# A two-layer encoder trunk on one core: the MLP's first tile pairs, its spills and its block order

## The chip, the cores and the metric

One Trainium2 chip, one of its cores. The metric is the device time of one launch in microseconds (us). The five engines are TensorE (PE, with its weight loads as PEld), VectorE (DVE), ScalarE (ACT), GpSimd (POOL) and SyncE (SP, which here issues every DMA).

## The reference, cut to what matters

```python
D_MODEL, SEQ, DEPTH, D_FF = 1024, 1024, 2, 4096
for l in range(DEPTH):
    h = rms_norm(x, norm1_g[l])
    ...                                   # attention and recurrence heads -> mixed
    x = x + jnp.einsum('bsc,cd->bsd', mixed, w_out[l])
    h2 = rms_norm(x, norm2_g[l])
    u = jax.nn.relu(jnp.einsum('bsd,df->bsf', h2, w_up[l]))
    x = x + jnp.einsum('bsf,fd->bsd', u * u, w_down[l])
return rms_norm(x, final_g)
```

Everything is float32. The change lies in the second half of a layer: the output projection's norm, the up product with its squared ReLU, and the down product.

## The kernel before, in words

Activations lie transposed, with 128 features on the partitions and the sequence along the free axis in two halves of 512 (`hf` 0 and 1). A float32 product is made of three matmuls: each operand is split into a rounded high part (`hi`) and the rest (`lo`), and hi·hi, hi·lo and lo·hi are added in PSUM. A split is one ACT cast and one DVE subtraction (L543 and L544 for activations, L599 and L600 for weights).

Both MLP products use Strassen's scheme in Winograd's form: 7 block products in place of 8. A left block A11 to A22 is 128x128 of weights, a right block B11 to B22 is 128x512 of activations; the row index is the feature block, the column index the half of the sequence. The weight sums S1 to S4 are formed on POOL in `lhs_forms` (L591 and L610), the activation sums T1 to T4 in `strassen_rhs` for the up product. `up_pair` makes a *pair* q, two 128-wide tiles of the 4096 hidden features; 16 pairs make the hidden layer. Its 7 products have 4 blocks of depth and 3 matmuls each: 84 matmuls. They run in the order A11·B11, A12·B21, S2·T2, S1·T1, S3·T3, S4·B22, A22·T4, on three accumulators `a`, `b`, `c` (PSUM tags `pa`, `mm`, `pr`). Partial sums leave `a` and `c` by `copy_out` (ACT, L640); `fin` finishes three of the four outputs with two DVE instructions (L655 adds, L656 does ReLU and square in one) and the fourth with two ACT instructions (L652, L653).

`spill(q, ...)` forms the T sums of the pair's squared outputs on POOL (L679 to L687) and writes all seven forms to DRAM (`us`). When all 16 pairs are done, the 16 x tiles are read back (L885), and the down product reads the forms with `fetch_rhs` (L694), seven per q, and splits them. A *block* (t, q0, n) of the down product (`down_pair`) adds n of the 16 depth steps to two tiles of the output: 7 products of 3n matmuls, each followed by one DVE addition into x (L705). A product on the same accumulator as the one before it waits until that addition has read it. The order is three short blocks (n = 1, 2, 3), twelve of n = 4, and four that close a row of tiles each: (0,12,4), (1,13,3), (2,14,2), (3,15,1). These four defer their S1 and S4 products (`tail`), so that the first half of x is finished first; `leave` then norms that half while the tails run.

The order of the instructions on each engine is fixed when the program is built: the instructions are placed in the order of the text, with those in `tc.high_priority()` first, by a model of when each is ready. An engine, and SP's queue of DMAs, then takes them strictly in that order. Tiles with the same tag share `bufs` slots: the tag `us` has 6 slots of 128x512, for partial sums, spilled sums and fetched forms. The split tiles of the up product's right side (B11[k], T2[k], ... for k = 0 to 3) are the same memory as those of the down product (`form_tiles(f, q % 4)`), so a fetched form can be split only when the last pair has read that form.

Of the kernel before, what the change touches and what calls it, by code (L numbers as in the profile page):

```python
# [38 lines left out]
US = 6  # L39


@with_exitstack
def trunk(ctx, tc, x, norm1_g, w_in, lam_qk, attn_norm_g, lb_logits, hgrn_norm_g,
# [136 lines left out]
    def sum_squares(sqp, xt, hf):  # L180
        acc = half(sqp, "sqa", 1)
        A.activation(acc, xt[0][hf], AF.Square)
        for b in range(1, NB):
            sq = half(sqp, "sq", 2)
# [13 lines left out]
    def norm_rows(sqp, xt, hf):  # L198
# [6 lines left out]
        inv_sqrt(R, acc, half(sqp, "sq", 2))  # L205
# [352 lines left out]
    def strassen_rhs(hst, h, mp):  # L558

        B = [{"B11": hst[k], "B21": hst[k + 4]} for k in range(4)]  # L560
        t2 = []
        for k in range(4):
            b11, b12, b21, b22 = h[k]
            V.tensor_tensor(b11, b12, b11, op=ALU.subtract)
            t = half(mp, "us", US)
            V.tensor_tensor(t, b22, b11, op=ALU.subtract)
            t2.append(t)
            B[k]["T2"] = split_into(form_tiles("T2", k, mp), t)
        for k in range(4):
            b11, b12, b21, b22 = h[k]  # L570
            B[k]["T1"] = split_into(form_tiles("T1", k, mp), b11)
        for k in range(4):
            b11, b12, b21, b22 = h[k]
            G.tensor_tensor(b12, b22, b12, op=ALU.subtract)
            B[k]["T3"] = split_into(form_tiles("T3", k, mp), b12)
        for k in range(4):
            B[k]["B22"] = split_into(form_tiles("B22", k, mp), h[k][3])
        for k in range(4):
            b21 = h[k][2]
            G.tensor_tensor(b21, b21, t2[k], op=ALU.subtract)  # L580
            B[k]["T4"] = split_into(form_tiles("T4", k, mp), b21)
        return B

    def lhs_forms(src, mp, view, n, part=0):

        with tc.high_priority():
            wr = mp.tile([P, 8, 256], F32, tag="wr", name="wr", bufs=2)
            dma(wr[:, :2 * n], src)
            v = wr[:, :2 * n].rearrange(view, i=2)
            c0, c1 = slice(0, P), slice(P, 2 * P)  # L590
            sub = lambda o, a, b: G.tensor_tensor(o, a, b, op=ALU.subtract)  # L591
            out = {}

            def group(names, x):
                m = len(names)
                hi = wp.tile([P, 1024], F32R, tag="whi", name="whi")
# [10 lines left out]
            sa, sb = stile(), stile()  # L607
            if part != 2:
                group(("A11", "A12"), v[:, :, :, c0])
            G.tensor_tensor(sa[:, 0], v[:, 0, :, c1], v[:, 1, :, c1], op=ALU.add)  # L610
            if part == 0:
                sub(sa[:, 1], sa[:, 0], v[:, 0, :, c0])
                group(("S1", "S2"), sa)
                sub(sb[:, 0], v[:, 0, :, c0], v[:, 0, :, c1])
                sub(sb[:, 1], v[:, 1, :, c0], sa[:, 1])
                group(("S3", "S4"), sb)
            elif part == 1:
                sub(sb[:, 0], sa[:, 0], v[:, 0, :, c0])
                sub(sb[:, 1], v[:, 0, :, c0], v[:, 0, :, c1])
                group(("S2", "S3"), sb)  # L620
            else:
                sub(sb[:, 0], sa[:, 0], v[:, 0, :, c0])
                sub(sa[:, 1], v[:, 1, :, c0], sb[:, 0])
                group(("S1", "S4"), sa)
            if part != 2:
# [3 lines left out]
    def product(ps, w, B, f, ks, start):  # L629
        n = len(ks)  # L630
        for j, k in enumerate(ks):
            hi, lo = B[k][f]
            for i, (lt, rt) in enumerate(((w[0], hi), (w[0], lo), (w[1], hi))):
                T.matmul(ps, lt[:, j], rt, start=(start and j + i == 0), stop=(j == n - 1 and i == 2),  # L634
                         skip_group_check=True)

    def copy_out(mp, ps):
        t = half(mp, "us", US)
        with tc.high_priority():
            A.copy(t, ps)  # L640
        return t

    def up_pair(w, B, q, xtile, mp):

        ks = range(4)
        o = [xtile(4 * (q // 2 % 2) + i, q % 2) for i in range(4)]
        a, b, c = pst("pa"), mmp.tile([P, HALF], F32, tag="mm", name="mm"), pst("pr")

        def fin(i, ps, x):
            with tc.high_priority():  # L650
                if x is None:
                    A.activation(o[i], ps, AF.Relu)  # L652
                    A.activation(o[i], o[i], AF.Square)  # L653
                else:
# [4 lines left out]
        p1 = copy_out(mp, a)  # L659
        product(b, w["A12"], B, "B21", ks, True)  # L660
        fin(0, b, p1)
        product(a, w["S2"], B, "T2", ks, False)
        p6 = copy_out(mp, a)
        product(c, w["S1"], B, "T1", ks, True)
        p5 = copy_out(mp, c)
        product(a, w["S3"], B, "T3", ks, False)
        fin(3, a, p5)
        product(c, w["S4"], B, "B22", ks, False)
        fin(1, c, p6)
        product(a, w["A22"], B, "T4", ks, False)  # L670
        fin(2, a, None)
        return o

    def spill(q, u, mp):
# [4 lines left out]
        G.tensor_tensor(t1, u12, u11, op=ALU.subtract)  # L679
        put("T1", t1)  # L680
        put("B22", u22)
        G.tensor_tensor(t2, u22, t1, op=ALU.subtract)
        put("T2", t2)
        G.tensor_tensor(u12, u22, u12, op=ALU.subtract)
        put("T3", u12)
        put("B21", u21)
        G.tensor_tensor(t4, u21, t2, op=ALU.subtract)  # L687
        put("T4", t4)

    def fetch_rhs(q, mp):  # L690
        r = {}
        for i, f in enumerate(FORMS):
            t = half(mp, "us", US)
            dma(t, us[:, q, i])  # L694
            r[f] = split_into(form_tiles(f, q % 4, mp), t)
        return r

    def down_pair(w, B, q0, n, xt, t, defer=False):
        ks = range(q0, q0 + n)
        a, b, c = pst("pa"), mmp.tile([P, HALF], F32, tag="mm", name="mm"), pst("pr")  # L700

        def add(i, hf, ps):
            x = xt[2 * t + i][hf]
            with tc.high_priority():
# [253 lines left out]
```

## Time and profile before

| | us |
|---|---|
| median of 3 runs (lowest, highest) | 2696.88 (2689.63, 2703.72) |
| the profiled execution | 2696.91 |
| its span, first to last instruction | 2695.1 |
| busy: PE, PEld | 2501.1, 2060.9 |
| busy: DVE, ACT, POOL | 1830.3, 1161.5, 825.9 |

The mean granted TensorE clock is 0.964 of full speed. PE is busy for 93% of the span; the MLP of the first layer lies between about 645 and 1355 us, that of the second between about 1979 and 2690 us. Busy time counts pipelined matmuls by their modelled ends, so where matmuls stand back to back their distance (start to start), not their duration, is their price.

### The profile page before, as it was taken

The page shows a single profiled execution, that of the slowest core. Times are in us where ns is not written, and L with a number is a line of the kernel's source. Part 1 is how long each engine was busy: PE and PEld are TensorE (multiplying, and loading weights), DVE is VectorE, ACT ScalarE, POOL GpSimd, SP SyncE. Part 2 cuts the span into 40 slices and gives each one's busy share as a digit, 9 for nine tenths or more (in the row PEclk, how much of TensorE's full clock was granted, in tenths as well). Part 3 has the DMA queues.
Part 4 walks back from the last instruction along what each step waited for, and adds up shares of the span by engine and source line. Part 5 has one row for each costly group of instructions (what it writes and reads, how often), then busy time and mean ns, then how long its engine had stood idle before and what let it go on. Part 6 is the DMA issues. An engine that isn't in the chain of part 4 may idle for free. (4 is left out here: it accounts for less than half of the span.)

```text
span 2695.1 us, 34858 instructions
## 1 busy us (share of the span) xinstructions
PE 2501.1 (93%) x12640; PEld 2060.9 (76%) x12640; DVE 1830.3 (68%) x3177; ACT 1161.5 (43%) x2271; POOL 825.9 (31%) x508
## 2 busy tenths in 40 slices
PE   8999999986999979999899999998969999799996
PEld 6877887875788857788688778877758888578875
DVE  5567566867655559887745775588775555688875
ACT  5455445644333334433434554456433333344432
POOL 1111111003667553333311111110037666333322
PEclk9999999988999989999999999999989999899998
DMA  7111111152344556443421111112714445654433
GB/s 235 42 52 44 52 44 48 59 191 83 131 151 147 168 200 192 138 152 117 140 60 48 40 44 44 48 48 62 228 47 141 154 145 174 210 168 154 144 98 113
DMA packets 255884, 306.85 MB, mean 114 GB/s; under 512 B 13968, under 2 KB 166844, under 8 KB 255712
## 3 DMA queue, kind: packets, MB, share of 16 engines
q1 hardware_dynamic: 255712, 304.63, 34.8%
q8 instruction: 99, 1.62, 0.2%
q14 instruction: 73, 0.60, 0.1%
HBM read 213.33 MB, written 89.41 MB: 112 GB/s over the span
## 5 line engine op out<-in xcount | busy, mean ns | idle before, releaser
L634 PE MATMUL pa<-T,whi 128*128 128x512 f32 x1536 | 488.2, 399 | 20.7 <-DVE x L705 18.1
L610 POOL TENSOR_TENSOR wst<-wr 128x512 f32<-128x512 f32 (+3 forms) x78 | 113.9, 1461 | 917.0 <-DVE wlo L129 293.7
L129 POOL TENSOR_TENSOR wlo<-wst,whi 128x1024 fp32r<-128x1024 f32 x56 | 138.2, 2468 | 815.3 <-ACT whi L127 791.5
L143 PE MATMUL mm<-hh,whi 128*128 128x512 f32 x896 | 364.4, 407 | 1.2 <-DVE ta L747 0.9
L143 PE MATMUL mm<-hh,wlo 128*128 128x512 f32 x896 | 363.4, 406 | 1.7 <-POOL wlo L129 1.7
L634 PEld LDWEIGHTS pa<-T,whi 128*128 128x128 f32 x1536 | 289.8, 190 | 94.9 <-DVE x L705 12.5
L143 PE MATMUL mm<-hl,whi 128*128 128x512 f32 x896 | 361.3, 404 | 0.0
L634 PE MATMUL pa<-T,wlo 128*128 128x512 f32 x768 | 304.7, 397 | 0.0
L599 ACT CAST whi<-wr 128x1024 fp32r<-128x1024 f32 (+5 forms) x140 | 109.0, 779 | 314.7 <-PE pr L634 271.5
L599 ACT CAST whi<-wst 128x1024 fp32r<-128x1024 f32 (+3 forms) x140 | 137.0, 979 | 232.7 <-PE mm L634 89.6
L600 DVE TENSOR_TENSOR wlo<-wst,whi 128x1024 fp32r<-128x1024 f32 (+3 forms) x140 | 207.4, 1481 | 41.2 <-ACT whi L599 41.2
L634 PE MATMUL pr<-hh,whi 128*128 128x512 f32 x512 | 207.6, 406 | 25.9 <-ACT hh L543 19.4
L634 PE MATMUL pr<-hl,whi 128*128 128x512 f32 x512 | 203.5, 397 | 21.4 <-DVE hl L544 21.4
L634 PE MATMUL pr<-hh,wlo 128*128 128x512 f32 x512 | 203.4, 398 | 0.0
L600 DVE TENSOR_TENSOR wlo<-wr,whi 128x1024 fp32r<-128x1024 f32 (+5 forms) x140 | 163.0, 1164 | 54.2 <-ACT whi L599 53.9
L143 PEld LDWEIGHTS mm<-hh,wlo 128*128 128x128 f32 x896 | 172.2, 192 | 36.0 <-POOL wlo L129 4.0
L143 PEld LDWEIGHTS mm<-hl,whi 128*128 128x128 f32 x896 | 173.4, 193 | 33.8 <-issue 1.2
L143 PEld LDWEIGHTS mm<-hh,whi 128*128 128x128 f32 x896 | 172.9, 193 | 34.3 <-DVE ta L747 1.7
L634 PEld LDWEIGHTS pa<-T,wlo 128*128 128x128 f32 x768 | 146.0, 190 | 35.0
L543 ACT CAST hh<-us 128x512 fp32r<-128x512 f32 x128 | 79.2, 620 | 185.6 <-PE pr L634 100.9
L221 PE MATMUL mm<-wlo,hh 128*128 128x256 f32 x512 | 147.7, 288 | 0.3 <-POOL wlo L129 0.3
L221 PE MATMUL mm<-whi,hh 128*128 128x256 f32 x512 | 148.0, 289 | 0.0
(242 smaller groups left out, 5697.9 us busy)
## 6 DMA issues: line engine op xcount, KB each, us to landing
us<-us SPq DMA_DIRECT2D x320, 256.0 KB, 2.6
wr<-w_up SPq DMA_DIRECT2D x32, 1024.0 KB, 5.7
us<-x SPq DMA_DIRECT2D x128, 256.0 KB, 2.3
wst<-w_in SPq DMA_DIRECT2D x56, 512.0 KB, 3.7
wr<-w_down SPq DMA_DIRECT2D x28, 1024.0 KB, 4.8
wst<-w_out SPq DMA_DIRECT2D x32, 512.0 KB, 4.0
x<-xs SPq DMA_DIRECT2D x64, 256.0 KB, 4.0
xs<-x SPq DMA_DIRECT2D x48, 256.0 KB, 2.7
```

The source lines that it names most:

```text
L129: eng.tensor_tensor(lo, st, hi.bitcast(F32), op=ALU.subtract)
L143: T.matmul(ps, lt[:, b], rt, start=(i == 0), stop=(i == n - 1))
L221: T.matmul(ps[:, t * 256:t * 256 + 256], lt[:, tsl], rt[:, b], start=(i + t + b + k == 0), stop=(i == 1 and b == 3 and k == 2), skip_group ...
L543: A.copy(hl[0], src)
L599: A.copy(hv, x)
L600: V.tensor_tensor(lv, x, hv.bitcast(F32), op=ALU.subtract)
L610: G.tensor_tensor(sa[:, 0], v[:, 0, :, c1], v[:, 1, :, c1], op=ALU.add)
L634: T.matmul(ps, lt[:, j], rt, start=(start and j + i == 0), stop=(j == n - 1 and i == 2), skip_group_check=True)
```

## The change

- The pairs q = 0 and 1 of the up product are no longer made by Strassen's 7 products but by the plain 8 (`up_plain`), first for half 0 of the sequence (4 products for each pair), then for half 1. Their splits of half 1 lie in the tiles of B22 and T4, the weights of the second pair in the tiles of T3.
- `strassen_rhs` and `spill` form their sums with DVE instructions in place of POOL's, in place.
- Of each up pair, all four outputs take ReLU and square on ACT; DVE keeps the three additions (`squared`).
- Four x tiles and the first four forms of q = 0 are loaded ahead of the last pair, through a new tag `uf` with 4 slots; the splits and fetches of q = 0 and 1 stand in the text ahead of the last pair's spill. The other x tiles come after it.
- The down product starts with (0,0,2) and then runs (1,0,1) and (2,0,3) together, product by product (`down_pairs`); at the end (1,13,3) and (2,15,1) run together, between (3,12,4) and (0,14,2). The twelve blocks of n = 4 take the row of tiles t in the order 3, 1, 0, 2.
- All x tiles come from one pool; the squares of the norms use the tag `us` instead of tiles of their own.

The diff, cut to its core:

```diff
 def strassen_rhs(hst, h, mp):
+    B = [{"B11": hst[k, 0], "B21": hst[k + 4, 0], "B22": hst[k + 4, 1]} for k in range(4)]
+    sub = lambda o, x, y: V.tensor_tensor(o, x, y, op=ALU.subtract)
     for k in range(4):
         b11, b12, b21, b22 = h[k]
-        V.tensor_tensor(b11, b12, b11, op=ALU.subtract)
-        t = half(mp, "us", US)
-        V.tensor_tensor(t, b22, b11, op=ALU.subtract)
...
-        G.tensor_tensor(b12, b22, b12, op=ALU.subtract)
...
-        G.tensor_tensor(b21, b21, t2[k], op=ALU.subtract)
+        sub(b11, b12, b11)
+        sub(b12, b22, b12)
+        sub(b22, b22, b11)
+        B[k]["T2"] = split_into(form_tiles("T2", k, mp), b22)
     for k in range(4):
+        B[k]["T1"] = split_into(form_tiles("T1", k, mp), h[k][0])
+    for k in range(4):
+        sub(h[k][2], h[k][2], h[k][3])
+    for f, i in (("T3", 1), ("T4", 2)):
+        for k in range(4):
+            B[k][f] = split_into(form_tiles(f, k, mp), h[k][i])
...
+def up_plain(w, B, sfx, o):
+    for m in (1, 2):
+        ps = pst("pa") if m == 1 else mmp.tile([P, HALF], F32, tag="mm", name="mm")
+        product(ps, w[f"A{m}1"], B, "B1" + sfx, range(4), True)
+        product(ps, w[f"A{m}2"], B, "B2" + sfx, range(4), False)
+        squared(o[m - 1], ps, None)
+
+def squared(o, ps, x):
     with tc.high_priority():
-        A.copy(t, ps)
...
-                if x is None:
-                    A.activation(o[i], ps, AF.Relu)
-                    A.activation(o[i], o[i], AF.Square)
-                else:
-                    V.tensor_tensor(o[i], ps, x, op=ALU.add)
-                    V.scalar_tensor_tensor(o[i], o[i], 0.0, o[i], op0=ALU.max, op1=ALU.mult)
+        if x is None:
+            A.activation(o, ps, AF.Relu)
+        else:
+            V.tensor_tensor(o, ps, x, op=ALU.add)
+            A.activation(o, o, AF.Relu)
+        A.activation(o, o, AF.Square)
...
 def spill(q, u, mp):
...
-    G.tensor_tensor(t1, u12, u11, op=ALU.subtract)
+    V.tensor_tensor(t1, u12, u11, op=ALU.subtract)
...
+def down_pairs(w, B, windows, xt, defer=False):
...
+    def step(bk, wf, f, start, i, hf):
+        off = 0
+        for j, (t, q0, n) in enumerate(windows):
+            product(ps[j, bk], w[wf], B, f, range(q0, q0 + n), start, off)
+            off += n
+            x = xt[2 * t + i][hf]
+            with tc.high_priority():
+                V.tensor_tensor(x, ps[j, bk], x, op=ALU.add)
...
         for b in (0, 4, 1, 5, 2, 6, 3, 7):
...
-                if hf == 0:
-                    hst[b] = split_into(h_tiles(b, 0), xt[b][0])
+                hst[b, hf] = split_into(h_tiles(b, 0) if hf == 0 else form_tiles("B22", b - 4, mp)
+                                        if b >= 4 else form_tiles("T4", b, mp), xt[b][hf])
...
+        wP = [up_forms(0, "AB"), up_forms(1, "AB", [3, 2, 1, 0])]
+        oP = [[half(mp, "uf", UF) for _ in range(2)] for _ in range(2)]
+        for q in range(2):
+            up_plain(wP[q], hP, "1", oP[q])
+        for q in range(2):
+            o = [half(mp, "us", US) for _ in range(2)]
+            up_plain(wP[q], hP, "2", o)
+            oP[q] = [oP[q][0], o[0], oP[q][1], o[1]]
         hB = strassen_rhs(hst, ..., mp)
+        for q in range(2):
+            spill(q, oP[q], mp)
...
-        for q in range(NF // 2):
...
+        for q in range(2, NF // 2):
+            if q == NF // 2 - 1:
+                for b in range(4):
+                    load_x(b)
+                st = {}
+                fetch_rhs(0, mp, None, st, FORMS[:UF], "uf")
+            u2 = up_pair(up_forms(q, "AS2"), hB, q, xtile, mp)
+            if q == NF // 2 - 1:
+                for i in range(2):
+                    uB[i] = {}
+                    split_rhs(i, mp, uB[i], st)
+                    fetch_rhs(i, mp, None, st, [f for f in FORMS if f not in uB[i]][:UF], "uf")
+                    split_rhs(i, mp, uB[i], st)
+                    if i == 0:
+                        fetch_rhs(1, mp, None, st, FORMS[:UF], "uf")
             spill(q, u2, mp)
...
-        steps = [(1, 0, 1), (2, 0, 2), (3, 0, 3)]
-        steps += [(r % 4, r, 4) for r in range(13)]
-        final = [(0, 12, 4), (1, 13, 3), (2, 14, 2), (3, 15, 1)]
+        steps = [[(0, 0, 2)], [(1, 0, 1), (2, 0, 3)]] + [[((3, 1, 0, 2)[r % 4], r, 4)] for r in range(12)]
+        final = [[(3, 12, 4)], [(1, 13, 3), (2, 15, 1)], [(0, 14, 2)]]
```

## Rows read from the trace of the kernel before

**Rows 1.** Windows: width; busy (count) PE, PEld, DVE, ACT, POOL; PEclk, DMA, GB/s

```profile
645.00:713.80 68.80, 47.67 (x187) 36.93 (x186) 51.71 (x64) 27.14 (x42) 35.41 (x20) 0.80 0.21 69
713.80:981.30 267.50, 267.50 (x1165) 218.28 (x1163) 151.55 (x139) 89.05 (x123) 174.24 (x113) 1.00 0.46 159
981.30:1050.80 69.50, 47.28 (x176) 33.62 (x175) 54.39 (x71) 30.19 (x49) 25.08 (x18) 0.88 0.65 212
1050.80:1282.80 232.00, 231.58 (x995) 185.98 (x996) 189.12 (x213) 92.86 (x129) 78.02 (x46) 1.00 0.45 141
1282.80:1340.00 57.20, 47.49 (x182) 34.88 (x180) 38.23 (x60) 20.20 (x35) 15.91 (x18) 0.91 0.39 129
1979.00:2047.00 68.00, 46.86 (x188) 36.41 (x187) 51.92 (x64) 27.68 (x43) 36.38 (x21) 0.82 0.21 70
2313.80:2385.00 71.20, 48.41 (x177) 34.63 (x176) 54.40 (x71) 30.25 (x49) 25.86 (x18) 0.86 0.63 207
2615.00:2655.00 40.00, 32.46 (x136) 23.25 (x134) 23.83 (x35) 10.38 (x17) 8.69 (x11) 0.96 0.28 93
```

**Rows 2.** TensorE's waits, 570 to 1400 us: total, times, longest (us)

```profile
PE pa L634 <- ACT hh L543: 14.3, 1, 14.3
PE pr L634 <- DVE hl L544: 10.7, 1, 10.7
PE pr L634 <- ACT hh L543: 9.7, 1, 9.7
PE pa L634 <- DVE x L705: 8.5, 8, 1.7
```

**Rows 3.** Timeline of VectorE and GpSimd, first layer's second norm: start, duration (us)

```profile
649.74 0.69 DVE L203 TENSOR_SCALAR sqa<-pa 128x512 f32<-128x512 f32 x1 [1.22 <-PE pa L202]
655.45 5.39 DVE L830 SCALAR_TENSOR_TENSOR x<-x,cols,R 128x512 f32<-128x512 f32 x8
661.52 4.67 POOL L574 TENSOR_TENSOR x<-x,x 128x512 f32<-128x512 f32 x2 [10.60 <-DVE x L564]
675.78 0.68 DVE L544 TENSOR_TENSOR hl<-x,hh 128x512 fp32r<-128x512 f32 x1
```

**Rows 4.** Timeline of SP's DMAs and ScalarE, last pair's end to first fetches

```profile
982.73 1.72 SPq L677 DMA_DIRECT2D us<-us  x2
987.93 0.32 SPq L677 DMA_DIRECT2D us<-us  x1
988.30 1.87 SPq L885 DMA_DIRECT2D x<-xs  x4
990.22 9.37 SPq L694 DMA_DIRECT2D us<-us  x10
995.29 1.25 ACT L543 CAST hh<-us 128x512 fp32r<-128x512 f32 x2 [12.24 <-DMA us<-us]
```

**Rows 5.** Groups of VectorE, 995.9 to 1050.8 us: busy (us), mean (ns), idle before

```profile
L544 DVE TENSOR_TENSOR hl<-us,hh 128x512 fp32r<-128x512 f32 x19 | 19.6, 1043 | 13.0 <-ACT hh L543 13.0
L544 DVE TENSOR_TENSOR T<-us,T 128x512 fp32r<-128x512 f32 x13 | 11.3, 870 | 0.0
```

**Rows 6.** Groups of VectorE, up pairs of the first layer, 713.8 to 981.3 us

```profile
L600 DVE TENSOR_TENSOR wlo<-wst,whi 128x1024 fp32r<-128x1024 f32 x27 | 48.5, 1795 | 14.4 <-ACT whi L599 14.4
L656 DVE SCALAR_TENSOR_TENSOR x<-x 128x512 f32<-128x512 f32 x42 | 39.7, 946 | 1.4
L655 DVE TENSOR_TENSOR x<-pa,us 128x512 f32<-128x512 f32 x14 | 9.7, 692 | 13.4 <-PE pa L634 13.4
```

**Rows 7.** Groups of ScalarE, the same stretch

```profile
L653 ACT ACTIVATE x<-x 128x512 f32<-128x512 f32 x13 | 8.2, 634 | 0.4
L652 ACT ACTIVATE x<-pa 128x512 f32<-128x512 f32 x13 | 7.6, 588 | 0.0
```

**Rows 8.** Timeline of VectorE and ScalarE, a pair's end and the last sums

```profile
941.60 1.22 DVE L600 TENSOR_TENSOR wlo<-wr,whi 128x1024 fp32r<-128x1024 f32 x1
...
944.42 0.63 ACT L653 ACTIVATE x<-x 128x512 f32<-128x512 f32 x1
...
2680.38 0.68 DVE L705 TENSOR_TENSOR x<-pr,x 128x512 f32<-128x512 f32 x1
2681.83 1.49 DVE L186 TENSOR_TENSOR sqa<-sqa,sq 128x512 f32<-128x512 f32 x2 [0.76 <-ACT sq L185]
```

More of the change, by code (lines that the diff above doesn't have):

```diff
@@ L204, in norm_rows @@
         R = rp.tile([P, HALF], F32, tag=f"R{hf}", name=f"R{hf}")
-        inv_sqrt(R, acc, half(sqp, "sq", 2))
+        inv_sqrt(R, acc, half(sqp, "us", US))
         return R
@@ L595, in group @@
                 m = len(names)
+                if held:
+                    for i, f in enumerate(names):
+                        hl = form_tiles("T3", held.pop(), mp)
+                        hl = split_into([t.rearrange("p (j c) -> p j c", c=P) for t in hl], x[:, i])
+                        out[f] = tuple(hl)
+                    return
                 hi = wp.tile([P, 1024], F32R, tag="whi", name="whi")
@@ L633, in product @@
             for i, (lt, rt) in enumerate(((w[0], hi), (w[0], lo), (w[1], hi))):
[L634 to L639, printed above, removed]
-            A.copy(t, ps)
-        return t
+                T.matmul(ps, lt[:, off + j], rt, start=(start and j + i == 0),
+                         stop=(j == n - 1 and i == 2), skip_group_check=True)
@@ L688, in spill, with fetch_rhs @@
         put("T4", t4)
[L690 to L704, printed above, removed]
-                V.tensor_tensor(x, ps, x, op=ALU.add)
-        def tail(w):
-            product(c, w["S1"], B, "T1", ks, True)
-            add(1, 1, c)
-            product(c, w["S4"], B, "B22", ks, False)
-            add(0, 1, c)
-        product(a, w["A11"], B, "B11", ks, True)
-        add(0, 0, a)
-        product(b, w["A12"], B, "B21", ks, True)
-        add(0, 0, b)
-        product(a, w["S2"], B, "T2", ks, False)
-        add(0, 1, a)
+    def fetch_rhs(q, mp, r, st, names, tag):
+        for f in names:
+            if st is not None:
+                st[f] = half(mp, tag, UF if tag == "uf" else US)
+                dma(st[f], us[:, q, FORMS.index(f)])
@@ new lines, in split_rhs, with tail @@
+    def split_rhs(q, mp, r, st):
+        for f in list(st):
+            r[f] = split_into(form_tiles(f, q % 4, mp), st.pop(f))
+    def down_pairs(w, B, windows, xt, defer=False):
+        bank = {"a": lambda: pst("pa"), "b": lambda: mmp.tile([P, HALF], F32, tag="mm", name="mm"),
+                "c": lambda: pst("pr")}
+        ps = {(i, k): bank[k]() for i in range(len(windows)) for k in ("ab" if defer else "abc")}
+        def step(bk, wf, f, start, i, hf):
[4 more added lines that the diff above has]
+                x = xt[2 * t + i][hf]
+                with tc.high_priority():
+                    V.tensor_tensor(x, ps[j, bk], x, op=ALU.add)
+        def tail(wl):
+            nonlocal w
+            w = wl
+            for j in range(len(windows)):
+                ps[j, "c"] = bank["c"]()
+            step("c", "S1", "T1", True, 1, 1)
+            step("c", "S4", "B22", False, 0, 1)
+        step("a", "A11", "B11", True, 0, 0)
+        step("b", "A12", "B21", True, 0, 0)
+        step("a", "S2", "T2", False, 0, 1)
@@ L900, in trunk @@
-        for (t, q0, n) in steps[:-1]:
-            while done < q0 + n:
-                fetch(done)
-                done += 1
-            down_pair(down_forms(t, q0, n), uB, q0, n, xt, t)
-        while done < NF // 2:
-            fetch(done)
-            done += 1
-        rest = []
-        for (t, q0, n) in final:
-            rest.append(down_pair(down_forms(t, q0, n, 1), uB, q0, n, xt, t, defer=True))
+            for i in range(len(uB), q):
+                uB[i] = {}
+                for j, f in enumerate(FORMS):
+                    st = {}
+                    fetch_rhs(i, mp, uB[i], st, [f], "uf" if j % 2 else "us")
+                    split_rhs(i, mp, uB[i], st)
@@ new lines, in trunk, with down_forms @@
+        for b in range(4, NB):
+            load_x(b)
+        def down_forms(windows, parts):
+            srcs = []
+            for t, q0, n in windows:
+                src = w_down[l][q0 * 256:(q0 + n) * 256, t * 256:t * 256 + 256]
+                srcs.append(src.rearrange("(b p) d -> p b d", p=P))
+            return lhs_forms(srcs, mp, "p (j i) c -> p i j c", parts)
+        steps = [[(0, 0, 2)], [(1, 0, 1), (2, 0, 3)]] + [[((3, 1, 0, 2)[r % 4], r, 4)] for r in range(12)]
+        final = [[(3, 12, 4)], [(1, 13, 3), (2, 15, 1)], [(0, 14, 2)]]
```

151 lines of the change are left out of this document (78 added, 73 removed).

## The prediction

> **What bounds the kernel now.** I read the table of busy shares first: TensorE is busy for 93% of the span, so the question is where it is not. The table of windows, cut at the stages of the MLP, answers it. In the up pairs and in the full blocks of the down product the matmuls stand back to back: the 14 pairs from 713.8 to 981.3 us are 14 × 84 = 1176 matmuls by the code (1165 are recorded) in 267.5 us, 0.2275 us each, 19.1 us a pair [rows 1]. Nothing that shortens DVE, ACT or POOL is worth anything there. The three other windows hold far fewer matmuls than their width; width less count × 0.2275 is what TensorE loses:
>
> - Start of the up product: 68.8 − 187 × 0.2275 = 26.3 us; in the second layer 68.0 − 188 × 0.2275 = 25.2 us [rows 1].
> - From the last up pair into the down product: 69.5 − 176 × 0.2275 = 29.5 us; in the second layer 71.2 − 177 × 0.2275 = 30.9 us [rows 1].
> - The closing blocks: 57.2 − 182 × 0.2275 = 15.8 us; in the second layer, where I cut earlier, 40.0 − 136 × 0.2275 = 9.1 us [rows 1].
>
> The list of TensorE's waits then names what ends them: 9.7 and 10.7 us for T splits, 14.3 us for the first split of a fetched form, and many small waits for the DVE addition that reads an accumulator [rows 2]. After each long wait the granted clock is under 1 for a while (0.80 and 0.88 as window means [rows 1]); the losses above include that.
>
> **Start of the up product.** The timeline shows why TensorE stands: half 1 gets its norm at 649.7, eight DVE scalings from 655.45, then sums and splits, with two POOL subtractions alone taking 4.67 us [rows 3]. Before, only the 24 matmuls of A11·B11 and A12·B21 need nothing of half 1. After, the plain products of half 0 for both pairs do not: 2 × 4 × 4 × 3 = 96 matmuls, 21.8 us. They start where the 24 start now, near the window's start at 645, pass the norm's matmul (about 1 us) and reach to about 668. By then half 1 must be split: 8 scalings (5.4 us) and 8 subtractions of 0.68 us from 655.45 end at 666.3; the first is there at about 657.5 (655.45, one scaling of 0.67, one cast of 0.63 [rows 4], one subtraction), and the products take them in the same order, so there is no wait. The plain products of half 1 last to 668 + 21.8 = 690. In that time DVE has 16 subtractions and 8 splits for T2 and T1: 24 × 0.68 = 16.3 us, from 666 to 683, plus weight splits of some 4 us: 687. T3 and T4 need tiles that are free only at 690, 8 more splits or 5.4 us; but S3·T3 is the fifth product, four products or 10.9 us later. So all of it is covered. The price is the eighth product: 2 pairs × 12 matmuls = 24 × 0.2275 = 5.5 us a layer. With 1 us left over the gain is 26.3 − 5.5 − 1 = 19.8 us, in the second layer 18.7: 38.5 us. Bounds of what is left over: 0.5 us (the norm's matmul) to 10.7 us (the longer of today's waits stays).
>
> **Into the down product.** SP's queue shows the order: the last pair's final form goes out at 987.93, because POOL forms it; behind it stand the last x loads at 988.30, behind them the first fetches at 990.22, and the first split starts at 995.29, 14 us after the last matmul [rows 4]. After, the first four forms of q = 0 are in SBUF before the last pair starts, and each is split as soon as that pair has read the tile it overwrites. B11 is free after the first product. The first matmul of the down product then follows the last pair at once, and the 14.3 us go. What is late next is DVE. From 995.9 to 1050.8 it works without a pause: 32 splits (30.9 us, mean 0.97), and additions and weights besides, some 52.5 of the window's 54.4 us [rows 1, 5]. After the change it must do the same work, less what moves under the last pair: six splits of q = 0 and two or three of q = 1, 8.5 × 0.97 = 8.2 us, plus four spill subtractions, 2.8 us. That is 47 us for 40.0 us of matmuls: 7 us lost, plus 3 us for the four waits on an accumulator in (0,0,2), where six matmuls (1.4 us) cover an addition of 0.69 us and its hand-over, and for the odd form still under way. I take 10 us lost a layer, so a gain of 19.5 and 20.9: 40.4 us. Bounds: 4 us lost if the splits fall from 0.97 to the 0.68 us that they take alone [rows 3, 5]; 20 us lost if nothing is split ahead of the last matmul but q = 0's first forms and the x loads still hold up the next fetches.
>
> **The closing blocks.** Fewer, fuller blocks: (1,13,3) and (2,15,1) alternate, so each covers the other's accumulator wait. TensorE waits 8.5 us in eight such waits in one layer, most of them here and in the short first blocks [rows 2]. I take 6 us in the first layer and 4 in the second, between nothing and 10 each. Against that stands the order of the sum of squares: it starts with tile 0 (`sum_squares`), and tiles 0 and 1 are now the last to be finished, where it was 6 and 7. The last addition of the program ends at 2681.06, and two sums later, at 2683.32, the chain is over [rows 8]. After, seven sums at some 0.7 us follow the square of tile 0: about 3 us more at the program's end, and I allow 1.5 us where the first layer passes into the second. Net 10 − 4.5 = 5.5 us.
>
> **Steady up pairs.** Three DVE instructions of 0.95 us a pair go (ReLU and square in one, 42 in 14 pairs), and four subtractions of 0.69 us come; ACT gets six instructions more, 3 × (0.588 + 0.634) = 3.7 us [rows 6, 7]. ACT is at 89.05 of 267.5 us and goes to 89.05 + 14 × 3.7 = 141 us, 53%; DVE keeps its 57%; POOL loses 4 subtractions a pair [rows 1]. All of it lies under the back-to-back matmuls, so the sum is 0; without that cover it would be 3.7 us a pair. Bounds: nothing to gain, since TensorE is never idle there; the loss is the third rival.
>
> The low parts of the weight sums take 1.80 us in the up pairs, and 1.22 us where POOL is not at work [rows 6, 8]. The Trainium skill (GPSIMD Engine Reference, Key points) says that GpSimd shares its SBUF interfaces with VectorE and contends with its instructions that have two SBUF inputs. By that, DVE's time in the up pairs falls by up to 0.58 us for each of these 27 instructions; TensorE is the bound there, so the sum would be the same.
>
> **The sum.** 38.5 + 40.4 + 5.5 = 84.4 us. The profiled execution is 2696.91 us (span 2695.1 and 1.8 around it), as good as the median of the runs, 2696.88. 2696.9 − 84.4 = 2612.5; I predict 2612 us, 3.1% faster. A measurement of this kernel can tell about 0.5%, 13 us, from no change.
>
> **The rivals.**
>
> *DVE holds the start of the down product.* Everything but the 14.3 us wait stays: 20 us lost there in place of 10 in each layer, 2612 + 20 = 2632. For it: DVE is already full in that stretch, and the first two blocks, now 2 and 4 wide, want 14 and then 7 splits at once. Against it: DVE is only 57% busy in the pair before, and the splits that can go there need nothing else.
>
> *The plain products cover nothing.* If half 1's splits or the second pair's weights stand behind something in their queue until the plain products of half 0 are long over, the wait only moves: the 38.5 us are not won, and the 24 matmuls of each layer are still paid, 11 us: 2612 + 49.5 = 2661. It begins to cost when the first half-1 split comes after 668 and has eaten the gain when it comes 19.8 us later, at 688; I expect it at 657.5. For it: the order on ACT before already puts a T3 cast, which waits for POOL, ahead of casts that were ready. Against it: the POOL step that misled that order is gone.
>
> *The spill on DVE stalls every pair (slower).* DVE takes its instructions in order. The last spill subtraction of a pair waits for the fourth output, which ACT squares after the pair's last matmul. If it stands ahead of the next pair's first weight split in DVE's order, that split slips. In the trace that split starts at 941.60, just before the pair's end, and the square at 944.42 [rows 8]. The square would end at 945.05, the subtraction at 945.74, and the split would start 4.1 us later than now; its lo part is wanted by the next pair's third matmul, which leaves some 0.4 us to spare. That is 3.7 us a pair, 28 × 3.7 = 104 us, 2612 + 104 = 2716, slower by 0.7%. It turns into no gain at 84.4 / 28 = 3.0 us a pair. For it: POOL could wait for that square at no cost, DVE can't, since weight splits and accumulator additions are queued behind. Against it: the split is in the high-priority part, the subtraction is not, and DVE is idle a third of the time there. The Trainium skill (ScalarE: Activation LUTs, Rules for kernel authors) says to put ReLU on VectorE, not on ScalarE; it speaks against the longer path from addition to square, and would make this rival likelier. The rows agree in size: 1.22 us of ACT replace 0.95 us of DVE [rows 6, 7].
>
> **How the numbers follow.** Forecast (2597 to 2630): 0.60. Better still (both starts at their low bound, and the closing blocks at theirs: 2612 − 12 − 6 = 2594): 0.05. DVE-held start (2622 to 2645): 0.17. Plain products cover nothing, or half: 0.08. Some stall of 2.5 to 3.5 us a pair, so that nothing is won: 0.05. The slower rival: 0.05. Faster is 0.60 + 0.05 + 0.17 + 0.08 = 0.90, same 0.05, slower 0.05. The range takes in the forecast, the DVE-held start and the nearer part of the cover rival: 2594 to 2650.
>
> **What would show it.** Right: in the new trace, no TensorE wait over 2 us between the output projection and the first pair by 7 products; the pairs at 19.1 us; no wait at the last pair's end, and DVE without a pause for some 45 us after it. Wrong: pairs longer than 19.5 us (the slower rival); a wait on the first T or half-1 split of 5 us and more (the cover rival); a first down block whose matmuls stop for fetched forms. The forecast is wrong altogether if the granted clock in the up pairs is no longer 1.00 with fewer pauses, for which no row speaks.

## The result

The changed kernel takes 2603.3 us (median of 4 runs, 2602.2 to 2613.7) against 2693.3 us for the kernel before on the same chip: a ratio of 0.967, 95% interval 0.963 to 0.971. It ran again with the last experiments, 2603.6 us against 2690.5, ratio 0.968 (0.966 to 0.970). The prediction was 2612 us, 2594 to 2650. The profiled execution is 2602.2 us, its span 2600.2, where before had 2695.1.

### The profile page after: what moved, and what is told of

Its sections match the earlier page's. It is cut to its first block, busy times and chain, and to the rows that moved or that the text cites. A ratio compares the mean times of both kernels' runs of the same rounds, so it can differ in the third digit from the quotient of the medians.

```text
span 2600.2 us, 34936 instructions
## 1 busy us (share of the span) xinstructions
PE 2476.9 (95%) x12688; PEld 2053.2 (79%) x12688; DVE 1837.1 (71%) x3201; ACT 1260.4 (48%) x2439; POOL 568.5 (22%) x328
## 5 line engine op out<-in xcount | busy, mean ns | idle before, releaser
L647 PE MATMUL pa<-T,whi 128*128 128x512 f32 x1456 | 459.1, 396 | 17.4 <-DVE x L735 12.1
L647 PEld LDWEIGHTS pa<-T,whi 128*128 128x128 f32 x1456 | 273.1, 189 | 86.4 <-DVE x L735 7.5
L620 POOL TENSOR_TENSOR wst<-wr 128x512 f32<-128x512 f32 (+1 forms) x56 | 100.9, 1801 | 914.5 <-DMA wr<-w_down 293.6
L647 PE MATMUL pa<-T,wlo 128*128 128x512 f32 x728 | 287.0, 394 | 0.0
L606 ACT CAST whi<-wst 128x1024 fp32r<-128x1024 f32 (+1 forms) x124 | 127.1, 1025 | 175.8 <-PE mm L647 88.6
L607 DVE TENSOR_TENSOR wlo<-wst,whi 128x1024 fp32r<-128x1024 f32 (+1 forms) x124 | 192.7, 1554 | 14.9 <-ACT whi L606 14.6
L606 ACT CAST whi<-wr 128x512 fp32r<-128x512 f32 (+2 forms) x128 | 105.1, 821 | 189.4 <-PE pr L647 134.7
L647 PE MATMUL pr<-hh,whi 128*128 128x512 f32 x480 | 191.7, 400 | 3.6 <-ACT whi L606 3.1
L607 DVE TENSOR_TENSOR wlo<-wr,whi 128x512 fp32r<-128x512 f32 (+2 forms) x128 | 120.9, 945 | 86.3 <-ACT whi L606 84.2
L512 ACT ACTIVATE s<-s,nm 128x256 f32<-128x256 f32 (+7 forms) x128 | 99.0, 774 | 109.2 <-DVE nm L507 105.0
```

The source lines that it names most:

```text
L512: A.activation(s[:, :nk], s[:, :nk], AF.Exp, bias=nm, scale=-1.0, accum_out=sm)
L606: A.copy(hv, x)
L607: V.tensor_tensor(lv, x, hv.bitcast(F32), op=ALU.subtract)
L620: G.tensor_tensor(sa[:, 0], a21, a22, op=ALU.add)
L647: T.matmul(ps, lt[:, off + j], rt, start=(start and j + i == 0), stop=(j == n - 1 and i == 2), skip_group_check=True)
```

## The profile after

The windows, cut at the same events as [rows 1] (first two pairs, 14 pairs, 69.5 us from the last pair on, closing blocks; then the second layer). The last row is the program's end. Columns: width; busy (count) of PE, PEld, DVE, ACT, POOL; granted clock, DMA share, GB/s.

```profile
639.20:684.40 45.20, 45.18 (x194) 36.52 (x195) 39.41 (x57) 24.79 (x42) 5.96 (x4) 1.00 0.28 94
684.40:954.80 270.40, 270.40 (x1177) 220.53 (x1177) 168.44 (x166) 145.16 (x217) 82.79 (x53) 1.00 0.48 167
954.80:1024.30 69.50, 61.26 (x248) 47.02 (x247) 64.94 (x78) 30.85 (x48) 26.60 (x16) 0.95 0.68 220
1236.70:1293.90 57.20, 48.59 (x199) 36.45 (x198) 42.82 (x56) 23.66 (x37) 17.98 (x14) 0.97 0.50 161
1916.20:1961.40 45.20, 45.20 (x194) 36.52 (x195) 39.27 (x57) 24.77 (x43) 6.18 (x4) 1.00 0.28 93
2231.90:2303.10 71.20, 62.74 (x250) 47.64 (x249) 65.62 (x79) 30.39 (x47) 24.71 (x16) 0.95 0.66 212
2515.00:2555.00 40.00, 30.42 (x136) 23.34 (x134) 22.95 (x29) 9.20 (x13) 11.58 (x10) 0.96 0.29 92
2555.00:2600.20 45.20, 26.18 (x120) 21.71 (x120) 24.77 (x43) 10.12 (x21) 7.18 (x6) 0.76 0.25 93
```

The start of the up product is full: 194 matmuls in 45.2 us, where 68.8 us held 187, and the granted clock is 1.00 all the time, the upper of TensorE's two levels (2.4 GHz; the lower, 1.2 GHz, shows as 0.50). The window behind the last pair holds 248 matmuls and not 176. The end of the second layer is the one place that is no better: 136 matmuls in 40 us as before, and then a mean clock of 0.76, so half of that stretch at the lower level.

TensorE's waits of the changed kernel, 570 to 1360 us, against [rows 2] (columns: total, times, longest):

```profile
PE pa L647 <- DVE x L735: 7.5, 8, 2.1
PE pr L647 <- ACT whi L606: 3.1, 2, 2.1
PE pa L175 <- DVE dg L174: 2.7, 2, 1.8
PE mm L647 <- DVE hl L545: 1.9, 1, 1.9
```

The waits of 14.3, 10.7 and 9.7 us are gone, and none over 2.1 us has come in their place. The second layer has two more, before the norm's matmuls at the end (2512 to 2601 us):

```profile
PE pa L195 <- DVE us L187: 16.5, 2, 11.3
PE pa L647 <- DVE x L735: 1.0, 2, 0.8
```

To set step against step I counted the MLP's matmuls of each layer in order of start (1344 + 1344 before, 1368 + 1344 after) and took the time between the same ones. "Output projection" runs from its first matmul to the first product; the last row runs on to the next layer's first dense_rows matmul, or to the end.

| stage, us before → after | first layer | second layer | predicted |
|---|---|---|---|
| output projection | 133.0 → 129.0 | 134.8 → 129.8 | 0 |
| first two pairs | 65.4 → 45.2 | 64.2 → 45.2 | −19.8, −18.7 |
| 14 pairs, to the first down matmul | 285.0 → 270.5 | 284.9 → 270.6 | with the next two rows −19.5, −20.9 |
| next 129 matmuls | 42.6 → 39.9 | 44.2 → 41.6 | |
| next 1005 | 236.2 → 233.8 | 234.3 → 233.4 | |
| closing blocks and what follows | 100.1 → 92.8 | 88.1 → 93.2 | −4.5, −1.0 |

The sum is −87.9 us. The span fell by 94.9; the other 7.0 lie in the two stages before an output projection, whose code is untouched. The second layer's took between 460.9 and 470.9 us in the profiles used here, so no cause is sought for them.

## The experiments

All edits are to the changed kernel. Times are medians; "changed" is 2603 us. The kernel before ran beside every experiment and took 2689.8 to 2690.8 us, so times from different chips are set beside each other.

**1. The first pairs by 7 products again.**

```diff
-        for q in range(2):
-            up_plain(wP[q], hP, "1", oP[q])
...
-        for q in range(2, NF // 2):
+        for q in range(NF // 2):
```

> The changed kernel with the first two pairs made by 7 products again, the sums still on VectorE and in place. Theory (the plain products of half 0 cover the norm and the sums of half 1): TensorE stands for 17 to 20 us per layer again and saves 5.5 us of matmuls, so 24 to 32 us more than the changed kernel, 2627 to 2635 us. Rival (what cost the time was GpSimd in the sums, and VectorE alone is quick enough): TensorE stands for under 12 us per layer and the kernel is within 10 us of the changed one.

2640.9 us (ratio to before 0.982, 0.979 to 0.984), 38 us more. The first two pairs take 65.8 and 65.6 us, as before the change. TensorE's waits of this kernel, 630 to 700 us:

```profile
PE pr L647 <- ACT hh L544: 11.5, 1, 11.5
PE pa L647 <- DVE wlo L607: 2.5, 1, 2.5
PE pa L647 <- ACT T L544: 1.6, 1, 1.6
```

One wait of 11.5 us has taken the place of two of 9.7 and 10.7, but the two pairs take as long as before the change, so sums on VectorE alone save nothing here: the plain products carry the gain. The waits add up to 17.9 us, inside the theory's 17 to 20. The kernel lost 6 us more than the upper end of that forecast because the theory left out the clock: the granted clock is 0.50, the lower level, from 649 to 669 us, a stretch that begins in the long wait, and 0.82 on average over the 65.8 us.

**2. No loads ahead of the last pair, then also no slots of their own.**

```diff
-                for b in range(4):
-                    load_x(b)
-                fetch_rhs(0, mp, None, st, FORMS[:UF], "uf")
...
-                    split_rhs(i, mp, uB[i], st)
...
-        for b in range(4, NB):
+        for b in range(NB):
             load_x(b)
```

> The changed kernel without the loads ahead of the last up pair: all sixteen x loads and every fetch stand behind the last spill again; the rest is as changed (sums on VectorE, blocks of 2 and 4 first). Theory (the queue of DMAs behind the last spill made the 14 us wait, and early fetches take it away): a wait of 11 to 14 us is back at the end of the last pair in each layer, and the two layers lose 25 to 36 us, 2630 to 2640 us. Rival (VectorE is the bound of that stretch, the wait is made good afterwards): under 12 us in all, below 2615 us. Rival (the quicker spill on VectorE was what mattered): the wait is under 6 us.

2619.1 us, 16 us more, with a wait of 9.8 us: between the theory and its first rival. The text alone does not hold the fetches back: four free slots let some of them be placed ahead of the spill anyway (in this kernel's queue they begin at 952.3 us, and the last spill goes out at 974.0). The second kernel takes the slots too:

```diff
-                    fetch_rhs(i, mp, uB[i], st, [f], "uf" if j % 2 else "us")
+                    fetch_rhs(i, mp, uB[i], st, [f], "us")
```

> As the kernel without the early loads, and all fetched forms in the six slots of the tag us: no fetch can take a slot that the last pair or its spill does not leave free. Without the early loads alone 16 us of the gain was lost and the wait at the last pair's end was 9.8 us, because some fetches into the four new slots still ran ahead of the spill. Theory (the slots let these fetches pass): the wait grows to 12 to 15 us, and the kernel takes 6 to 14 us more than without the early loads, 2625 to 2633 us. Rival (the slots do not matter): within 4 us of 2619 us.

2628.4 us, another 9 us, as the theory had it, and the wait is nearly what it was. TensorE's waits of this second kernel, 690 to 1010 us:

```profile
PE pa L647 <- ACT hh L544: 14.4, 3, 13.3
```

Early loads and slots together are worth 25 us by the medians, 21 us of them in the stages of the table. The stage of the 14 pairs goes from 270.5 to 284.0 us, nearly as long as before the change (285.0), while the next 129 matmuls get 2 to 4 us shorter. That VectorE catches up in the pause would explain the latter; no run shows it.

**3. The old order of blocks.**

```diff
-        steps = [[(0, 0, 2)], [(1, 0, 1), (2, 0, 3)]] + [[((3, 1, 0, 2)[r % 4], r, 4)] for r in range(12)]
-        final = [[(3, 12, 4)], [(1, 13, 3), (2, 15, 1)], [(0, 14, 2)]]
+        steps = [[(1, 0, 1)], [(2, 0, 2)], [(3, 0, 3)]] + [[(r % 4, r, 4)] for r in range(12)]
+        final = [[(0, 12, 4)], [(1, 13, 3)], [(2, 14, 2)], [(3, 15, 1)]]
```

> The changed kernel with the block order of before: (1,0,1), (2,0,2), (3,0,3) first, twelve full blocks with t = 0, 1, 2, 3, and (0,12,4), (1,13,3), (2,14,2), (3,15,1) last, each block alone. Tiles 6 and 7 are then finished last and the norm's sums, which run from tile 0, fit that order. Theory: 4 to 8 us lost at the start of the down product and 4 to 6 in the closing blocks of each layer, 12 to 16 us won back at the program's end; within 8 us of the changed kernel, and the two waits of 11.3 and 5.2 us at the end are gone. Rival (twos are worth nothing): 8 us or more less than the changed kernel, below 2595 us. Rival (the start needs the blocks of 2 and 4): over 2613 us.

2619.7 us: the last rival. The 129 matmuls take 48.0 and 49.6 us, 8 us more each. TensorE's longest wait there (940 to 1030 us) and the timeline of VectorE show a reason that none of the three named:

```profile
PE pr L647 <- DVE x L735: 11.6, 1, 11.6
```

```profile
978.15 1.88 DVE L545 TENSOR_TENSOR hl<-uf,hh 128x512 fp32r<-128x512 f32 x3
985.02 0.69 DVE L735 TENSOR_TENSOR x<-pr,x 128x512 f32<-128x512 f32 x1 [4.99 <-DMA x<-xs]
```

The blocks behind the first add into tiles 4 to 7, which are loaded after the last spill; an addition waits for such a load (5.0 us here), and TensorE for the addition, 11.6 us. The changed kernel begins with tiles 0 to 3, loaded early, and comes to tiles 4 and 5 later. So what the old order costs at the start is not shown to be its narrow blocks; the row of tiles that they begin with is in it. The waits of 11.3 and 5.2 us at the end are gone, as expected, but the stage wins back less than the 12 to 16 us: the closing blocks take 99.2 us in the first layer, 6.4 more than in the changed kernel, and 88.6 in the second, 4.6 less. So the new closing blocks are worth something by themselves.

**4. The order of the sum of squares, and a version with one more edit.**

```diff
-        A.activation(acc, xt[0][hf], AF.Square)
-        for b in range(1, NB):
+        A.activation(acc, xt[bs[0]][hf], AF.Square)
+        for b in bs[1:]:
...
+        acc = sum_squares(sqp, xt, hf, ((6, 7, 2, 4, 3, 5, 0, 1), (7, 6, 3, 5, 2, 4, 1, 0))[hf])
```

> The changed kernel with one edit: the norms at the end of a layer add the squares of the x tiles in the order in which the closing blocks finish them (6, 7, 2, 4, 3, 5, 0, 1 for half 0; 7, 6, 3, 5, 2, 4, 1, 0 for half 1) and not from tile 0 on. Theory (the order of the sum is the mis-sized term): the waits of 11.3 and 5.2 us before the norm's matmuls at the program's end fall to about 2 us each, in all 12 to 13 us less than the changed kernel, 2590 us. Rival (ACT holds the first of the two, because a weight cast that waits for GpSimd stands among its squares): the 11.3 us stay above 7, only the last wait shrinks, 3 to 4 us less, 2599 us.

2598.9 us. Both waits before the norms are under 1 us, as the theory had it, and the last row of the table falls from 93.2 to 82.6 us in the second layer. The median shows only 4 of these 11 us and so lies where the rival put it; its runs lie between 2593.0 and 2604.5. In the profiled one, stages that the edit leaves alone are longer: the output projections by 2.9 and 0.9 us, the stage between them by 3.8. A new wait has come: TensorE stood 5.8 us for L915, which reads a transposed tile out of PSUM. So one edit more:

```diff
-                    if c == 3:
+                    if c == 3 or (hf == 0 and i):
                         pp = mmp.tile([P, HALF], F32, tag="mm", name="mm")
```

> The kernel with the sums in the order of completion and one more edit: of half 0's last transposes those that took PSUM slots of the tag pr take slots of mm, so that the closing products of half 1, which accumulate in pr, need not wait for them. Theory (the new 5.8 us wait in the run with the sum order is for a pr slot held by a transpose that waits for the norm): that wait falls under 2 us, 3 to 5 us less than with the sum order alone, 11 to 16 us less than the changed kernel in the sums of the stages. Rival (the weight sums on GpSimd, which end late, hold the closing products as well): the wait stays at 4 us or more.

2589.3 us (4 runs; 2587.0 to 2591.1), ratio to before 0.962 (0.961 to 0.964), beside 0.968 (0.966 to 0.970) for the changed kernel on the same chip: 14 us faster, the best version of this study. The last row of the table is 77.7 us in the second layer, 15.5 less than in the changed kernel. TensorE's waits of this kernel, 2500 to 2590 us:

```profile
PE pa L647 <- DVE x L735: 4.0, 6, 0.9
PE pr L647 <- ACT whi L606: 2.0, 1, 2.0
```

**5. The spill's sums on GpSimd, then T3's and T4's too.**

```diff
-        V.tensor_tensor(t1, u12, u11, op=ALU.subtract)
+        G.tensor_tensor(t1, u12, u11, op=ALU.subtract)
...
-            sub(b12, b22, b12)
+            G.tensor_tensor(b12, b22, b12, op=ALU.subtract)
```

> The changed kernel with the four spill sums of every pair on GpSimd again. Theory (in the pairs nothing but TensorE counts, and at the last pair's end the early fetches keep the spill off the path): within 6 us of the changed kernel, 2600 to 2608 us, the pairs still 19.1 us each. Rival (the spill's engine counts, because the x loads and the next fetches stand behind the last spill): 5 to 8 us more per layer, 2613 to 2619 us.

The execution that was profiled took 10,247 us, so its trace says nothing of the stages; the three others took 2604.5, 2605.1 and 2616.0 us, ratio 0.970 (0.967 to 0.972), which can't be told from the changed kernel.

> The changed kernel with GpSimd for the four spill sums of every pair and for the sums of T3 and T4 (first kind of strassen_rhs), as before. It replaces the run with the spill alone on GpSimd, whose profile was disturbed. Theory (both starts have cover, the pairs have slack): the start of the two first pairs within 2 us of 45.2, the pairs within 1 us, the first down blocks 2 to 5 us longer per layer since the last spill is later; 2603 to 2613 us in all. Rival (sums on VectorE carry the gain at the start): the first pairs over 50 us per layer, 2615 us and more.

2621.3 us, 18 us more. Both sides missed: the time lies in the rival's range, but not for its reason. The first two pairs take 45.2 us, so GpSimd in those sums costs nothing there. The 14 pairs take 283.1 us, 12.6 more, and the 129 matmuls after them 36.5, 3.4 less. TensorE has two waits in the stage of the 14 pairs, and the timelines of ScalarE and VectorE show what stands behind them; the rest of the 12.6 us goes with a granted clock of 0.98 in place of 1.00.

```profile
PE pa L647 <- ACT us L659: 4.1, 1, 4.1
```

```profile
PE pa L647 <- DVE x L691: 3.9, 1, 3.9
```

```profile
699.76 0.58 ACT L659 COPY us<-pa 128x512 f32<-128x512 f32 x1 [4.19 <-DMA us<-us]
```

```profile
966.55 0.69 DVE L545 TENSOR_TENSOR hl<-uf,hh 128x512 fp32r<-128x512 f32 x1 [5.17 <-ACT hh L544]
967.16 0.68 DVE L691 TENSOR_TENSOR x<-pa,us 128x512 f32<-128x512 f32 x1
```

In the first of the 14 pairs a partial sum waits for a slot of `us` that a late spill still holds. In the last one a split of a fetched form stands in VectorE's order ahead of an addition that frees an accumulator, and its fetch is late (ScalarE's cast for it waits 5.2 us for the DMA). The run before this one differs by T3 and T4 alone and took 16 us less; how these two sums bring the waits stays open.

**6. ReLU and square on VectorE.**

```diff
-                A.activation(o, o, AF.Relu)
-            A.activation(o, o, AF.Square)
+                V.scalar_tensor_tensor(o, o, 0.0, o, op0=ALU.max, op1=ALU.mult)
```

> The changed kernel with ReLU and square of three of each pair's four outputs in one VectorE instruction again, in place of two on ScalarE. Theory (nothing but TensorE counts in the pairs): within 5 us of the changed kernel, pairs of 19.1 us. Rival (VectorE, which now also makes the spill's sums, has no room): the pairs grow by 0.3 us or more each, over 8 us in all.

2613.2 us, ratio 0.972 (0.969 to 0.975): the rival's size. This interval just overlaps that of the changed kernel; the stages carry the verdict. The 14 pairs take 276.9 and 276.5 us, 0.4 us a pair more. TensorE's waits of this kernel, 690 to 955 us, a stretch in which the changed kernel has none:

```profile
PE pa L647 <- DVE wlo L607: 4.2, 8, 0.5
```

Over the same stretch VectorE is busy for 190.35 of 265 us, 72%, so it is not full. In eight of the 14 pairs a weight's low part, which the pair's third matmul reads, comes half a microsecond late, and the pair takes 20.1 us and not 19.3. The timelines of VectorE and GpSimd around the start of a pair without the wait (723.0 us) and one with it (742.3) show the difference:

```profile
721.78 1.22 DVE L607 TENSOR_TENSOR wlo<-wr,whi 128x1024 fp32r<-128x1024 f32 x1
...
740.49 0.69 DVE L693 SCALAR_TENSOR_TENSOR x<-x 128x512 f32<-128x512 f32 x1
741.10 2.33 DVE L607 TENSOR_TENSOR wlo<-wr,whi 128x1024 fp32r<-128x1024 f32 x1
743.36 1.79 DVE L700 TENSOR_TENSOR us<-x,x 128x512 f32<-128x512 f32 x1
```

```profile
722.01 2.16 POOL L620 TENSOR_TENSOR wst<-wr 128x512 f32<-128x512 f32 x1 [10.29 <-DMA wr<-w_up]
...
741.04 1.31 POOL L620 TENSOR_TENSOR wst<-wr 128x512 f32<-128x512 f32 x1 [9.97 <-DMA wr<-w_up]
```

The split takes 1.22 us, but 2.33 where GpSimd's sum of weights began just ahead of it, 0.06 to 0.18 us in all eight pairs with the wait. In the others GpSimd began later, at most 0.02 us ahead, or not at all. The ReLU and square ahead of the split (L693) puts its start 1.22 us before the pair; in the changed kernel it is 1.71 us, in every pair before GpSimd begins. In the kernel before, the same instruction stood there, but GpSimd came to that sum later. So it is not shown that VectorE had no room; what the trace shows is a split that meets GpSimd. No run separates the two.

**7. The output projection, whose matmuls the change leaves as they were.**

> The changed kernel with the squares of the norm of half 0 before the up product in two slots of their own and one for the sum, as in the kernel before. It asks for the 3 us wait before that norm's matmul that the prediction did not foresee to go. Theory (with two slots ACT's squares wait for the sums on VectorE, so the sum is late): the wait of about 3 us and the slow matmuls behind it are back in each layer, 8 to 11 us more than the changed kernel, 2611 to 2614 us. Rival (the slots do nothing; another edit placed the norm's matmul later among the next half's): no wait, within 4 us.

The edit gives `sum_squares` of half 0 two slots for squares and one for the sum. 2605.2 us, the output projection 129.5 and 129.8 us: the slots are not it. The wait in question, in the kernel before (570 to 720 us):

```profile
PE pa L202 <- DVE sqa L186: 2.9, 1, 2.9
```

```diff
-            return xp.tile([P, HALF], F32, tag=f"x{b}_{hf}", name=f"x{b}_{hf}")
+            return (mp if hf else xp).tile([P, HALF], F32, tag=f"x{b}_{hf}", name=f"x{b}_{hf}")
```

> The changed kernel with the x tiles of half 1 from the MLP's pool again, which opens only when the recurrence's tiles are given back; the rest as changed. It asks for the 4 to 5 us per layer that the output projection takes less than before, which the prediction did not foresee and which the slots of the squares do not explain. Theory (with the early pool the next half's products can be placed ahead of the norm's matmul): the wait of 3 us before that matmul is back, the output projection takes 133 us and not 129, 8 to 10 us more in all. Rival (the placement follows from another edit): no wait, within 4 us of the changed kernel.

2629.8 us, 26 us more, and another wait than the one expected (TensorE's waits, 500 to 720 us, and SP's queue):

```profile
PE mm L144 <- DVE x L850: 11.8, 1, 11.8
```

```profile
610.36 4.70 SPq L846 DMA_DIRECT2D x<-xs  x6
```

The output projection takes 142.9 and 145.1 us, longer than before the change: the loads of half 1's x tiles go out only from 610.36, the first lands at 618.0, and at 618.1 VectorE makes the addition that needs it and empties an accumulator of the output projection. Three weight splits stand ahead of that addition in VectorE's order and end just then as well. The one pool of all x tiles is thus worth 13 to 15 us a layer in the changed kernel. What it explains of the 4 to 5 us against the kernel before stays open: there the squares lay in another pool, and the wait was another one. The 4 to 5 us themselves rest on one profile of the kernel before (133.0 and 134.8 us); in the kernels here that leave this stage as the change made it, it took 128.0 to 131.9.

> The changed kernel itself again, on the same chip as the others of this call, as the level against which their few microseconds are read: 2600 to 2610 us, with the attention stages some 5 us longer or shorter than in the first profile.

This is the second run of the changed kernel, 2603.6 us.

## Why the prediction was right

**Start of the up product.** Predicted −19.8 and −18.7 us, measured −20.2 and −19.0. The timeline of VectorE shows the cover as it was worked out:

```profile
642.47 0.69 DVE L204 TENSOR_SCALAR us<-pa 128x512 f32<-128x512 f32 x1 [1.44 <-PE pa L203]
...
648.23 2.99 DVE L857 SCALAR_TENSOR_TENSOR x<-x,cols,R 128x512 f32<-128x512 f32 x3
651.14 0.68 DVE L545 TENSOR_TENSOR T<-x,T 128x512 fp32r<-128x512 f32 x1
...
681.58 2.50 DVE L545 TENSOR_TENSOR T<-x,T 128x512 fp32r<-128x512 f32 x4 [0.34 <-ACT T L544]
```

The plain products of half 0 last from 639.2 to 662.3; the first split of half 1 is ready at 651.8, and the last T splits run at the end of the plain products of half 1 (684.4) and just behind it, four products ahead of S3·T3. Experiment 1 takes the plain products away, and the waits and the 65 us return; experiment 5 puts T3's and T4's sums back on GpSimd, and the 45.2 us stay. The rival that the plain products cover nothing is dead.

**Into the down product.** Predicted −19.5 and −20.9, measured −19.6 and −17.8 (rows three to five of the table). The named steps hold one by one: the wait of 14.3 us goes, experiment 2 brings it back, eight splits run before the last pair ends where 8.5 were counted on, and what is late next is VectorE. Its groups from 954.8 to 1009.7 us, against [rows 5] (columns: busy, mean ns, idle before):

```profile
L545 DVE TENSOR_TENSOR hl<-uf,hh 128x512 fp32r<-128x512 f32 x11 | 11.2, 1027 | 0.6 <-ACT hh L544 0.6
L735 DVE TENSOR_TENSOR x<-pa,x 128x512 f32<-128x512 f32 x14 | 9.6, 686 | 1.7 <-PE pa L647 1.4
...
L545 DVE TENSOR_TENSOR T<-us,T 128x512 fp32r<-128x512 f32 x8 | 7.0, 883 | 0.0
```

The first 129 matmuls would take 29.3 us back to back (129 × 0.2275) and take 39.9 and 41.6: 10.6 and 12.3 us lost, where 10 were predicted. In the first layer 6.0 us of them are waits, all for VectorE; most of the rest goes with a granted clock of 0.91. The rival that put 20 there is not borne out, but it was near: without the early loads and the slots the wait takes 13.3 us again, and with the old order of blocks the 129 matmuls take 8 us more.

**Closing blocks.** Net 5.5 us predicted, 2.2 measured (−7.3 and +5.1). The term that was mis-sized is the order of the sum of squares, priced at 3 us for the program's end. Undoing it gives back 10.6 us in the second layer's stage, and 15.5 with the transposes' slots as well. The blocks themselves did what was asked of them: with the sum in order the stage is 9.1 and 5.5 us shorter than before the change (100.1 → 91.0, 88.1 → 82.6), where 6 and 4 were predicted. VectorE and ScalarE in the changed kernel show what the price left out:

```profile
2582.09 5.47 DVE L187 TENSOR_TENSOR us<-us 128x512 f32<-128x512 f32 x7 [1.22 <-ACT us L186]
```

```profile
2547.66 1.67 ACT L186 ACTIVATE us<-x 128x512 f32<-128x512 f32 x3 [2.35 <-DVE x L735]
2553.52 1.04 ACT L606 CAST whi<-wst 128x1024 fp32r<-128x1024 f32 x1 [4.18 <-POOL wst L592]
2554.47 2.19 ACT L186 ACTIVATE us<-x 128x512 f32<-128x512 f32 x4
```

At the very end seven sums follow tile 0's square, about as priced: 5.5 us, where two took 1.49. But half 0's norm has the same chain, and the forecast had no term for it: its matmul stands in TensorE's order ahead of the closing products of half 1, which begin only at 2564.5, and TensorE stood 11.3 us for it. Among its squares ScalarE holds a weight cast that waits 4.2 us for GpSimd, the rival of experiment 4. That experiment does not separate the two, for in its kernel the same cast has come to stand behind the last square:

```profile
2555.50 0.63 ACT L186 ACTIVATE us<-x 128x512 f32<-128x512 f32 x1 [2.34 <-DVE x L735]
2560.78 1.04 ACT L606 CAST whi<-wst 128x1024 fp32r<-128x1024 f32 x1 [4.64 <-POOL wst L592]
```

An estimate from the changed kernel's rows: VectorE's third sum ends at 2552.4 and the fourth begins at 2555.7, so the cast can account for some 3.4 of the 11.3 us and the chain of sums for the rest.

**Steady pairs.** Predicted at 0, and they are (270.5 us, against 285.0 less the 14.3 us wait). Two readings on the way were off. The window from 713.8 us begins 2.8 us into the first of the 14 pairs, whose first matmul is at 710.99, so its 1165 matmuls are not 1176 with some missing from the record: the matmuls stand 0.230 us apart and a pair takes 19.3 us, before and after. That moves each of the losses by at most 0.5 us. And VectorE did not keep its 57%: it is busy for 62% of the pairs, because two of the four new subtractions took 1.61 and 1.67 us and not 0.69, and the low parts of the weight sums still take 1.67 us, with GpSimd at work for 83 of the 270 us. Neither cost anything under the matmuls.

The slower rival, a weight split late behind the spill's sums, did not happen. Experiment 6 has a late weight split, at 0.4 us a pair, but by another way: there the spill's sums stand behind the split (743.36 after 741.10), and it is late only where it meets GpSimd. The Trainium skill (ScalarE: Activation LUTs, Rules for kernel authors) puts ReLU on VectorE. The run here that is nearest to that, ReLU and square of three outputs on VectorE, took 10 us longer.

**Not foreseen:** 9 us in the output projection (experiment 7) and 7.0 us in stages whose code is untouched. Both helped, and that is luck: without them the forecast of −84.4 us stands against a measured −78.9. Of this difference the closing blocks account for 3.3 and the down product for about 3 (37.4 of 40.4 us); the start of the up product gave 0.7 more than was asked.

## What to carry to other kernels

A wait at a stage boundary can be paid for in work that needs only the finished half: here 5.5 us of additional matmuls took away 25 us of waiting and slow matmuls. When the order in which tiles are finished is changed, look at every reduction that runs over them in a fixed order: here one cost 10.6 us, because the matmul that waits for it stands on TensorE ahead of work that was ready. The place of an early load in the text is only part of it: with the place given up, four slots of their own still kept 9 of the 25 us.

## What the hardware showed that was not expected

The same VectorE instruction, the split of a 128x1024 weight tile, took 1.22 us and, where a GpSimd sum had begun 0.06 to 0.18 us ahead of it, 2.33 us (experiment 6, first layer: eight of 13 pairs, and no pair of the kernels before and after). That, and not a full engine, is what the trace shows where VectorE cost TensorE time at 72% busy, beside 62% in the changed kernel (159.92 of 260 us): a start half a microsecond later put the split behind GpSimd's sum, and with a fixed order the room that counts is that ahead of one deadline, here a weight's low part at a pair's start.
